# ScalarE and VectorE take the program's own order through the whole of a two-layer encoder kernel

## The chip, the cores and the metric

The kernel runs on one core of a Trainium2 chip. The metric is the device time of one execution in microseconds (us). Before the change it is 2368.7 us, the median of 3 runs (2365.86 to 2369.22). In the texts PE is TensorE (PEld its weight loads), DVE is VectorE, ACT is ScalarE, POOL is GpSimd and SP is the engine that issues the loads.

## What is computed

The input is 256 tokens of width 2048 in float32. Two layers run one after the other:

```
h = x
layer 0: h += windowed attention(rms_norm(h)) @ a_w_o     # 32 query heads of 64, 4 key heads, a sink logit, ALiBi, QK-norm
layer 1: h += differential attention(rms_norm(h)) @ b_w_o # 8 heads, each with two softmax maps of width 128
each:    h += (silu(g) * u) @ w_ffn_out,  [g, u] = rms_norm(h) @ w_ffn_in        # 5632 wide
         h += rms_norm(p[i] @ ple_w_proj) * sigmoid(rms_norm(h) @ ple_w_gate)
```

All weights (some 425 MB) are read once, and the result must be as exact as a float32 product.

## The kernel before

**Products.** A float32 operand is split in two parts, `hi` (rounded to the type that PE multiplies fast) and `lo` (the rest), and a product is three matmuls: x.hi with w.hi, x.lo with w.hi, x.hi with w.lo (`Group.tile`, L173; the matmul is L176). Weights come by DMA as `raw` tiles of 128 rows by 4 pieces of 256 columns, twice; `split_block` (L134 to L140) makes from half of one a `ws` tile: ACT casts `hi` (L138), DVE subtracts to get `lo` (L139). One `ws` tile serves 12 matmuls of 512 columns: two row blocks k, two token blocks m, three products. There are four `ws` buffers, and `Feed.next` (L198) keeps splits for four tiles emitted: when a tile is taken, the one three places on has just been written down in the program.

**Groups.** `Group.run` (L150) multiplies 16 row blocks (or fewer) into two PSUM tiles and then calls `done`. For queries and keys `done` is `qk_norm` (L367): squares on ACT (L374), sums on DVE (L375), a chain of seven small operations on POOL for the inverse root (L217 to L225, L378), and two multiplies on DVE that give `qn` (L388).

**Pieces.** What else a head needs is cut in pieces that `Flow` (L43) mixes into the stream of matmuls, a step after each matmul, each at a due time that a piece before has set: `to_pairs` (transposes, L398, then `qT` or `qk` split on ACT and DVE at L210 and L211), `scores` (L408), `exps` (L411 to L427: on DVE `sc`, L417, and `nm`, L419; on ACT two exponentials `e`, L423; on DVE `rd`, L426), `keys_first` (transposes of `e`, L437, then `wT` split at L206 and L207) and `weigh` (L521 in layer 0, L607 in layer 1). Layer 0 has 16 pairs of heads, each with two `exps` in a row (`AttentionA.heads`, L488). Layer 1 has 8 heads with two score maps each (`AttentionB.scores`, L571), taken in four rounds of two heads; the second map ends in a scaling on POOL (L582) and a sum on DVE (L584). PSUM tiles for pieces (`at`) come from a ring of four: scores of one pair can only start when DVE has read what stood there.

**Order.** PE's order is by hand for the whole program: it runs as the program emits it. ACT and DVE are by hand only up to the end of the first group (the `with` at L808); from L819 on a scheduler of the toolchain sets the order in which their instructions stand in their queues, as it does for POOL and SP throughout. On the chip each of these queues is taken in the order that stands there. `small_vectors` (L337) and `minus_lambda` (L351), both emitted early in the second group, turn small parameter vectors on PE and make one number for layer 1 with a matmul at L353.

Of the kernel before, what the change touches and what calls it, by code (L numbers as in the profile page):

```python
# [34 lines left out]
WS_BUFS = 4  # L35
# [50 lines left out]
def encoder(ctx: ExitStack, tc: tile.TileContext, x, p, attn_norm, ffn_norm, a_w_qkv, a_q_norm,  # L86
# [20 lines left out]
    flow = Flow()  # L107
# [535 lines left out]
    def project(w, os, norm):  # L643

        def done(half, s):
            def add(ps):
                add_to_h(ps, s)
                if half == 1:
                    norm.add(s, 3.0)
            return add  # L650
        n = KT // 2

        class Half:
            def __len__(self):
                return max(0, len(os) - n)

            def __getitem__(self, k):
                return os[n + k]
        return [Group(w, half * n * P, n, s, (os, Half())[half], done(half, s))
                for half in range(2) for s in range(NS)]  # L660
# [122 lines left out]
    groups = attn_a.groups() + project(a_w_o[0], attn_a.os, norm)  # L783
# [6 lines left out]
    feed = Feed(groups)  # L790
# [17 lines left out]
    with tc.manual_schedule(engines={mybir.EngineType.Activation, mybir.EngineType.DVE}):  # L808
# [6 lines left out]
        first_ps = groups[0].run(feed)  # L815
        for q in range(NS):
            feed.split()
            norm_a.stat.add([h[:, m, q * W:(q + 1) * W] for m in range(NM)])
    feed.ahead = WS_BUFS  # L819
    first_done(first_ps)  # L820
    flow.later(3.0, small_vectors)
    for g in groups[1:]:
        g.run(feed)
    flow.finish()
    phases.close()


# [49 lines left out]
```

## Time and profile before

| | |
|---|---|
| median of 3 runs | 2368.7 us |
| profiled execution, its own time | 2368.39 us |
| span of its trace, first to last instruction | 2366.6 us |
| PE busy | 2339.1 us, 99% |
| DVE busy | 1345.3 us, 57% |
| ACT busy | 1117.6 us, 47% |
| POOL busy | 138.6 us, 6% |
| layer 0 attention, in the trace | 28 to about 263 us |
| layer 1 attention, in the trace | about 1168 to 1470 us |

A busy PE is one with a matmul under way; matmuls overlap, so a busy stretch says only that PE had no empty time. The waits of an engine are listed by what ended them; a wait for several things is put down to the one that came last. The order in which instructions stand on an engine is printed from the built program and holds no time.

### The profile page before, as it was taken

What the parts mean: (1) busy time and instruction counts of PE and PEld (TensorE: products, weight loads), DVE (VectorE), ACT (ScalarE), POOL (GpSimd) and SP (SyncE); (2) the same over time, 40 slices, a digit from 0 to 9 for tenths busy, and PEclk for the clock granted to TensorE, in tenths of its full rate; (3) what the DMA queues carried; (4) which work ended last, traced back from release to release, by engine and by line L of the source; (5) the groups of instructions that cost most, each with busy time, mean ns of one, the idle gap of its engine ahead of it and who ended that gap; (6) DMA issues with size and microseconds to landing.
All of it is one profiled execution on the core that took longest, in us unless ns stands there. A gap on an engine that the chain in (4) does not pass through costs nothing.

```text
span 2366.6 us, 28473 instructions
## 1 busy us (share of the span) xinstructions
PE 2339.1 (99%) x10853; PEld 1920.7 (81%) x10853; DVE 1345.3 (57%) x1550; ACT 1117.6 (47%) x1551; POOL 138.6 (6%) x309
## 2 busy tenths in 40 slices
PE   8999999999999999999999999999999999999999
PEld 6777788888888888888888888888888888888887
DVE  5668655555555454566567667655545554454564
ACT  5555554444434434455455555544444434434453
POOL 1332000000000000000121120000000000000000
PEclk9999999999999999999999999999999999999999
DMA  6433455555555555555545445555555555555554
GB/s 236 143 107 107 165 182 191 188 196 187 193 185 191 192 188 192 193 178 184 194 159 178 162 168 193 178 187 184 200 184 201 183 195 192 189 189 196 180 196 141
DMA packets 121570, 428.72 MB, mean 181 GB/s; under 512 B 13552, under 2 KB 16728, under 8 KB 121176
## 3 DMA queue, kind: packets, MB, share of 16 engines
q1 hardware_dynamic: 121432, 426.89, 51.6%
q8 instruction: 85, 1.39, 0.2%
q14 instruction: 53, 0.43, 0.1%
HBM read 424.74 MB, written 2.10 MB: 180 GB/s over the span
## 4 chain that ended last, share of the span: by engine, by line
PE 96%; DVE 1%; DMA 1%; POOL 1%; ACT 1%; issue 1%; SPq 0%; DVEq 0%; ACTq 0%; POOLq 0%
PE mm L176 91%; PE at L408 1%; PE at L720 1%; PE at L269 1%; DMA h<-in_x_dram 1%; PE at L521 1%; PE at L437 1%; PE at L607 1%; PE at L398 0%; DVE ws L139 0%; POOL rs_y L219 0%; ACT ws L138 0%; DVE sc L417 0%; DMA raw<-in_a_w_qkv_dram 0%; DVE nm L419 0%
## 5 line engine op out<-in xcount | busy, mean ns | idle before, releaser
L176 PE MATMUL mm<-ws,xt 128*128 128x512 f32 x9600 | 2302.8, 397 | 6.1 <-DVE xt L207 4.2
L176 PEld LDWEIGHTS mm<-ws,xt 128*128 128x128 f32 x9600 | 1791.0, 188 | 405.8 <-DVE xt L207 5.4
L139 DVE TENSOR_TENSOR ws<-raw,ws 128x1024 fp32r<-128x1024 f32 x800 | 977.9, 1226 | 871.2 <-ACT ws L138 870.6
L138 ACT CAST ws<-raw 128x1024 fp32r<-128x1024 f32 x800 | 840.3, 1052 | 1035.9 <-PE mm L176 963.9
L217 POOL TENSOR_SCALAR rs_v<-ssum 128x2 f32<-128x2 f32 x8 | 1.5, 191 | 1708.0 <-DVE ssum L246 1708.0
L298 DVE TENSOR_TENSOR h<-mm,h 128x512 f32<-128x512 f32 x96 | 61.8, 682 | 1.5 <-PE mm L176 1.5
L210 ACT ACTIVATE xt<-at,gains 128x256 fp32r<-128x256 f32 x96 | 44.2, 473 | 33.1 <-DVE xt L211 23.9
L206 ACT CAST xt<-at 128x256 fp32r<-128x256 f32 x108 | 37.9, 372 | 42.7 <-DVE xt L207 31.8
L269 PE MATMUL at<-ident,h 128*128 128x128 f32 x192 | 52.6, 287 | 4.9 <-DMA h<-in_x_dram 4.8
L423 ACT ACTIVATE e<-sc,nm 128x257 f32<-128x257 f32 (+1 forms) x96 | 47.8, 501 | 15.4 <-DVE nm L419 15.4
L211 DVE SCALAR_TENSOR_TENSOR xt<-at,gains,xt 128x256 fp32r<-128x256 f32 x96 | 44.8, 480 | 17.9 <-ACT xt L210 17.9
L207 DVE TENSOR_TENSOR xt<-at,xt 128x256 fp32r<-128x256 f32 x108 | 43.2, 418 | 12.6 <-ACT xt L206 12.6
L521 PE MATMUL at<-wT,vp 128*128 128x256 f32 x192 | 47.4, 281 | 0.9 <-DVE sc L417 0.9
L720 PE MATMUL at<-ident,hid 128*128 128x128 f32 x176 | 47.8, 272 | 0.0
L219 POOL TENSOR_TENSOR rs_y<-rs_v,halves 128x2 f32<-128x2 f32 (+2 forms) x29 | 46.0, 1587 | 2.3
L437 PE MATMUL at<-ident,e 128*128 128x128 f32 x160 | 44.1, 277 | 0.0
L388 DVE TENSOR_TENSOR qn<-mm,rr 128x512 f32<-128x512 f32 (+1 forms) x28 | 16.9, 647 | 44.8 <-POOL rr L378 44.8
L701 ACT ACTIVATE silu<-mm,rinv 128x512 f32<-128x512 f32 x44 | 29.9, 688 | 19.7 <-PE mm L176 19.7
L521 PEld LDWEIGHTS at<-wT,vp 128*128 128x128 f32 x192 | 33.5, 189 | 1.8 <-ACT e L423 1.1
L501 POOL TENSOR_SCALAR e<-e,rd 128x256 f32<-128x256 f32 x64 | 33.6, 538 | 14.0 <-DVE rd L426 12.4
L269 PEld LDWEIGHTS at<-ident,h 128*128 128x128 f32 x192 | 27.7, 147 | 8.2 <-DMA h<-in_x_dram 5.4
L206 ACT CAST wT<-at 128x512 fp32r<-128x512 f32 x40 | 22.9, 580 | 23.5 <-PE at L437 23.4
(93 smaller groups left out, 652.0 us busy)
## 6 DMA issues: line engine op xcount, KB each, us to landing
raw<-in_w_ffn_in_dram SPq DMA_DIRECT2D x352, 512.0 KB
raw<-in_w_ffn_out_dram SPq DMA_DIRECT2D x176, 512.0 KB
raw<-in_b_w_qkv_dram SPq DMA_DIRECT2D x96, 512.0 KB
raw<-in_ple_w_gate_dram SPq DMA_DIRECT2D x64, 512.0 KB
raw<-in_a_w_qkv_dram SPq DMA_DIRECT2D x40, 512.0 KB
raw<-in_a_w_o_dram SPq DMA_DIRECT2D x32, 512.0 KB
raw<-in_b_w_o_dram SPq DMA_DIRECT2D x32, 512.0 KB
raw<-in_ple_w_proj_dram SPq DMA_DIRECT2D x16, 256.0 KB
```

Source lines behind the costliest of these rows:

```text
L138: nc.scalar.copy(out=ws[:, 0], in_=src)
L139: nc.vector.tensor_tensor(out=ws[:, 1], in0=src, in1=ws[:, 0].bitcast(F32), op=ALU.subtract)
L176: nc.tensor.matmul(ps[m], x[:, a, mslice(m)], w, start=(k == 0 and i == 0), stop=(k == self.n - 1 and i == 2))
L206: nc.scalar.copy(out=hi, in_=src)
L211: nc.vector.scalar_tensor_tensor(out=lo, in0=src, scalar=scale, in1=hi.bitcast(F32), op0=ALU.mult, op1=ALU.subtract)
L219: nc.gpsimd.tensor_tensor(out=y, in0=v, in1=halves[:, :n], op=ALU.pow)
L269: nc.tensor.transpose(ps[:, j, mslice(m)], h[:, m, (k + j) * P:(k + j + 1) * P], ident)
L298: nc.vector.tensor_tensor(out=hs, in0=ps[m], in1=hs, op=ALU.add)
L423: nc.scalar.activation(out=e[:, m, :], in_=sc[:, m, :], func=AF.Exp, bias=nm[:, m:m + 1], accum_out=den[:, m:m + 1])
L437: nc.tensor.transpose(ps[:, kh, mslice(m)], w[:, m, kh * P:(kh + 1) * P], ident)
L521: nc.tensor.matmul(ps, v[:, a, c0:c0 + P], wT[:, b, kh, :], start=(n == 0), stop=(n == 11))
L720: nc.tensor.transpose(ps[:, j, mslice(m)], hid[m][:, (j0 + j) * P:(j0 + j + 1) * P], ident)
```

## The change

The block in which ACT and DVE follow the program's order is carried on to the last instruction. Nothing that is computed changes, nor do the tiles, the buffers or the loads.

```
@@ -816,12 +816,12 @@
         for q in range(NS):
             feed.split()
             norm_a.stat.add([h[:, m, q * W:(q + 1) * W] for m in range(NM)])
-    feed.ahead = WS_BUFS
-    first_done(first_ps)
-    flow.later(3.0, small_vectors)
-    for g in groups[1:]:
-        g.run(feed)
-    flow.finish()
+        feed.ahead = WS_BUFS
+        first_done(first_ps)
+        flow.later(3.0, small_vectors)
+        for g in groups[1:]:
+            g.run(feed)
+        flow.finish()
     phases.close()
```

PE's order is the same in both. POOL's differs in one place (a scaling of `e` stands ahead of a root instead of behind it), SP's in the place of one load of layer 1. On ACT and DVE three places matter below.

The first is DVE behind the group of keys and values of layer 0, where `small_vectors` falls (`lp` is what the matmul at L353 reads). Before:

```order
L246 TENSOR_REDUCE ssum<-nss 128x2
L341 COPY gains<-at 128x64
L342 COPY cols<-at 128x10
L345 TENSOR_SCALAR gq_a<-cols 128x1
L345 TENSOR_SCALAR gq_b<-cols 128x1
L139 TENSOR_TENSOR ws<-raw,ws 128x1024
L375 TENSOR_REDUCE ss<-sq 128x4 x2
L345 TENSOR_SCALAR subln<-cols 128x2
L348 TENSOR_TENSOR lp<-cols 128x2
L388 TENSOR_TENSOR qn<-mm,rr 128x4x64 x4
```

There `lp` stands ahead of the multiplies `qn`. The same place of DVE after the change:

```order
L246 TENSOR_REDUCE ssum<-nss 128x2
L375 TENSOR_REDUCE ss<-sq 128x4 x2
L388 TENSOR_TENSOR qn<-mm,rr 128x4x64 x4
L211 SCALAR_TENSOR_TENSOR vp_436<-mm,rinv,vp_436 128x4x64
L211 SCALAR_TENSOR_TENSOR vp_440<-mm,rinv,vp_440 128x4x64
L139 TENSOR_TENSOR ws<-raw,ws 128x1024
L341 COPY gains<-at 128x64
L342 COPY cols<-at 128x10
L345 TENSOR_SCALAR gq_a<-cols 128x1
L345 TENSOR_SCALAR gq_b<-cols 128x1
L345 TENSOR_SCALAR subln<-cols 128x2
L348 TENSOR_TENSOR lp<-cols 128x2
```

Now `lp` and the copies it comes from stand behind `qn`, the two halves of the values (`vp`) and a weight split.

The second is DVE in layer 0 behind the second group of queries, with the scores of the second pair of heads. Before:

```order
L211 SCALAR_TENSOR_TENSOR qT<-at,gq_a,qT 128x2x256
L375 TENSOR_REDUCE ss<-sq 128x8 x2
L139 TENSOR_TENSOR ws<-raw,ws 128x1024
L388 TENSOR_TENSOR qn<-mm,rr 128x512 x2
L417 SCALAR_TENSOR_TENSOR sc<-dist,at 128x2x256 x2
L419 TENSOR_REDUCE nm<-sc 128x2 x2
L139 TENSOR_TENSOR ws<-raw,ws 128x1024
L426 RECIPROCAL rd<-den 128x2
L207 TENSOR_TENSOR wT<-at,wT 128x512
```

There a weight split stands in the gap ahead of `qn`, and both heads are read out of PSUM one right behind the other. The same place of DVE after the change:

```order
L211 SCALAR_TENSOR_TENSOR qT<-at,gq_a,qT 128x2x256
L375 TENSOR_REDUCE ss<-sq 128x8 x2
L388 TENSOR_TENSOR qn<-mm,rr 128x512 x2
L139 TENSOR_TENSOR ws<-raw,ws 128x1024
L417 SCALAR_TENSOR_TENSOR sc<-dist,at 128x2x256
L419 TENSOR_REDUCE nm<-sc 128x2
L426 RECIPROCAL rd<-den 128x2
L417 SCALAR_TENSOR_TENSOR sc<-dist,at 128x2x256
L419 TENSOR_REDUCE nm<-sc 128x2
L426 RECIPROCAL rd<-den 128x2
L139 TENSOR_TENSOR ws<-raw,ws 128x1024
L207 TENSOR_TENSOR wT<-at,wT 128x512 x2
```

The weight split has moved behind `qn`, and the second head's `sc` behind the first head's `rd`, which reads what ACT's exponentials of the first head leave.

The third is DVE in layer 1, where the second head of a round has its two score maps while the first head's `wT` is due. Before:

```order
L417 SCALAR_TENSOR_TENSOR sc<-dist,at 128x512 x2
L419 TENSOR_REDUCE nm<-sc 128x2 x2
L139 TENSOR_TENSOR ws<-raw,ws 128x1024
L426 RECIPROCAL rd<-den 128x2
L207 TENSOR_TENSOR wT<-at,wT 128x512
L426 RECIPROCAL rd<-den 128x2
L580 TENSOR_SCALAR r2l<-rd,nlam 128x2
L584 SCALAR_TENSOR_TENSOR e<-e,rd 128x256 x2
```

There `wT` stands between the two `rd`. The same place of DVE after the change:

```order
L417 SCALAR_TENSOR_TENSOR sc<-dist,at 128x512
L419 TENSOR_REDUCE nm<-sc 128x2
L426 RECIPROCAL rd<-den 128x2
L417 SCALAR_TENSOR_TENSOR sc<-dist,at 128x512
L419 TENSOR_REDUCE nm<-sc 128x2
L426 RECIPROCAL rd<-den 128x2
L580 TENSOR_SCALAR r2l<-rd,nlam 128x2
L584 SCALAR_TENSOR_TENSOR e<-e,rd 128x256 x2
L139 TENSOR_TENSOR ws<-raw,ws 128x1024
L207 TENSOR_TENSOR wT<-at,wT 128x512
```

Now `wT` stands behind both maps of the other head, their sum and a weight split; ACT's exponentials stand in the same way ahead of its half of `wT`.

## Rows read from the trace of the kernel before

**Rows 1.** The page, part 1: busy time, share and count by engine.
```profile
PE 2339.1 (99%) x10853; PEld 1920.7 (81%) x10853; DVE 1345.3 (57%) x1550; ACT 1117.6 (47%) x1551; POOL 138.6 (6%) x309
```

**Rows 2.** What PE waited for, 62 to 265 us: us, times, longest.
```profile
PE at L408 <- DVE xt L207: 4.5, 1, 4.5
PE mm L176 <- DVE xt L207: 4.2, 3, 2.6
```

**Rows 3.** Busy time by stretch (from:to, length; count of instructions behind x).
```profile
62.00:263.00 201.00, 186.61 (x1067) 149.26 (x1065) 141.91 (x219) 108.75 (x236) 60.40 (x122) 0.97 0.35 122
1168.00:1470.00 302.00, 301.97 (x1475) 249.71 (x1474) 201.63 (x273) 158.87 (x264) 48.35 (x113) 1.00 0.49 168
```

**Rows 4.** Groups by line and shape: busy us, mean ns of one.
```profile
L138 ACT CAST ws<-raw 128x1024 fp32r<-128x1024 f32 x800 | 840.3, 1052 | 1035.9 <-PE mm L176 963.9 <-issue 48.0 <-DVE sc L417 9.6
...
L211 DVE SCALAR_TENSOR_TENSOR v<-mm,rinv,v 128x256 fp32r<-128x256 f32 x16 | 7.3, 474 | 0.0
...
L211 DVE SCALAR_TENSOR_TENSOR qk<-at,cols,qk 128x512 fp32r<-128x512 f32 x8 | 6.0, 745 | 0.4 <-ACT qk L210 0.4
```

**Rows 5.** Instructions in time behind the first group: start, length, engine.
```profile
45.42 0.16 DVE L348 TENSOR_TENSOR lp<-cols 128x2 f32<-128x2 f32 x1
...
46.21 0.28 PE L353 MATMUL at<-lp,ones 128*128 128x2 f32 x2
...
48.88 1.42 DVE L388 TENSOR_TENSOR qn<-mm,rr 128x256 f32<-128x256 f32 x4 [3.31 <-POOL rr L378]
```

**Rows 6.** Instructions in time around the first query group's end.
```profile
59.69 15.38 PE L176 MATMUL mm<-ws,xt 128*128 128x512 f32 x67
...
63.84 1.23 DVE L139 TENSOR_TENSOR ws<-raw,ws 128x1024 fp32r<-128x1024 f32 x1 [0.25 <-ACT ws L138]
...
69.34 1.29 DVE L388 TENSOR_TENSOR qn<-mm,rr 128x512 f32<-128x512 f32 x2 [4.27 <-POOL rr L378]
```

**Rows 7.** Instructions in time at the second and third pair's scores.
```profile
94.14 1.29 DVE L388 TENSOR_TENSOR qn<-mm,rr 128x512 f32<-128x512 f32 x2 [4.58 <-POOL rr L378]
95.34 1.28 DVE L417 SCALAR_TENSOR_TENSOR sc<-dist,at 128x512 f32<-128x512 f32 x2
96.08 0.38 PE L408 MATMUL at<-kd,qT 64*128 64x256 f32 x1 [2.35 <-DVE sc L417]
...
97.31 0.51 ACT L423 ACTIVATE e<-sc,nm 128x257 f32<-128x257 f32 x1 [4.81 <-DVE nm L419]
...
98.22 0.18 ACT L423 ACTIVATION_READ_ACCUMULATOR e<-sc,nm 128x1 f32 x1
```

**Rows 8.** Busy time by stretch, for the granted clock (third number from the right).
```profile
96.50:100.00 3.50, 3.32 (x17) 2.71 (x18) 3.28 (x8) 2.69 (x10) 1.40 (x3) 0.68 0.00 0
100.00:104.00 4.00, 4.00 (x19) 3.32 (x19) 4.00 (x6) 2.40 (x8) 1.52 (x5) 0.86 0.00 0
...
135.50:139.00 3.50, 3.44 (x16) 2.81 (x17) 3.50 (x7) 0.00 (x0) 0.00 (x0) 0.50 0.00 0
139.00:143.00 4.00, 4.00 (x16) 2.87 (x15) 2.35 (x4) 2.20 (x5) 0.00 (x0) 0.61 0.00 0
...
180.00:184.00 4.00, 3.23 (x18) 2.61 (x19) 3.42 (x6) 1.83 (x3) 0.00 (x0) 1.00 0.28 67
```

**Rows 9.** Instructions in time in layer 1, second round.
```profile
1276.66 0.69 DVE L417 SCALAR_TENSOR_TENSOR sc<-dist,at 128x512 f32<-128x512 f32 x1 [0.44 <-PE at L408]
...
1282.72 0.94 POOL L582 TENSOR_SCALAR e<-e,r2l 128x256 f32<-128x256 f32 x2 [19.87 <-DVE r2l L580]
1283.24 1.09 DVE L584 SCALAR_TENSOR_TENSOR e<-e,rd 128x256 f32<-128x256 f32 x2 [0.30 <-POOL e L582]
...
1284.51 0.87 PE L408 MATMUL at<-qk,qk 128*128 128x256 f32 x6
...
1292.15 0.69 DVE L207 TENSOR_TENSOR wT<-at,wT 128x512 fp32r<-128x512 f32 x1
...
1292.89 0.38 PE L607 MATMUL at<-v,wT 128*128 128x256 f32 x1
```

## The prediction

> **What bounds the kernel now.** The page comes first: PE is busy for 2339.1 of 2366.6 us, DVE for little over half [rows 1]. So the change can only take away the few waits that PE has, or add new ones, and the second view is the list of PE's waits: in layer 0's attention it waits once for 4.5 us and three times, 4.2 us together, for an `xt` that DVE splits [rows 2]. The third view, busy time by stretch, tells where there is room. In layer 0's attention DVE works 141.9 of 201 us, at the granted clock of 0.97; in layer 1's PE works without a break [rows 3]. In the feed-forward stages, which the change leaves in nearly the same order (one `xt` moves past one weight split), I cost it at nothing: three tiles of splits lie ready there, 36 matmuls, and 67 matmuls run in 15.38 us [rows 6], 0.23 us each, so 8.2 us of cover.
>
> The fourth view is the instructions in time at the places where the order moves, and from it the durations are taken. The sum is made against the profiled execution's own 2368.4 us, 1.8 us more than its span and 0.3 us below the median of the runs.
>
> **The change, part by part.** Nothing is added but waiting. A queue that stands in the program's order meets each result at the moment it is made: DVE stands still while POOL makes a root and while ACT makes exponentials, and what would have filled the gap stands behind.
>
> *The start.* PE's matmul at L353 begins at 46.21, just after `lp` at 45.42 [rows 5]. Now `lp` stands behind `qn`, which ends at 48.88 + 1.42 = 50.30 because POOL makes the root until then [rows 5]. Behind it come the value halves (on ACT until about 50.8), the cast of a weight tile (1.05, [rows 4]) and its `lo` (1.23, as in [rows 6]), which ends at 53.1, and six small operations of about 0.15 (as `lp`, [rows 5]): 54.0. PE comes to L353 at the same time as before, so it waits 54.0 - 46.2 = 7.8 us. No other matmul stands between that could be done.
>
> *Layer 0's first query group.* The `lo` that ran at 63.84, in the gap before `qn`, now runs behind `qn`'s end at 70.63 and is there at 71.86 [rows 6]. The group ends near 61.7, the tile is due 36 matmuls later and its `lo` with the third product: 61.7 + 8.2 + 0.4 = 70.3. PE waits 1.6 us.
>
> *Layer 0's pairs of heads.* Before, both `sc` take 1.28 us together [rows 7], and both `nm` as much. Now the second head waits for the first: `sc` and `nm` 1.28, a step of 0.14, two exponentials from 97.31 to 98.40 [rows 7], 1.09, and `rd` with its step 0.28, 2.8 us for a head and 5.6 for a pair, against 2.9 of work: 2.7 us of standing still for each of 16 pairs. The first place where this reaches PE is the third pair's scores, which wait for the second pair's `sc` to leave PSUM and did so already before, until 96.08 [rows 7]. The first pair's 5.6 us hold ACT and so the next `qT`, the squares and with them `qn` by 2.3 us; with the 1.6 above `qn` ends at 95.43 + 3.9 = 99.3. Then a `lo` (1.2), the first head (2.8) and the second `sc` (0.64): 104.0, where it was 95.34 + 1.28 = 96.6 [rows 7]. That is 7.4 us, the 1.6 among them. Such a queue (two pairs' 2.7 and a `lo` of 1.2, 6.6 us) stands ahead of PE at four more places by the order and the waits: the scores that waited 4.5 us, and the three matmuls that waited for `xt`, the last at the end of the pairs [rows 2]. I take them all, 7.4 + 4 x 6.6 = 34 us. From below, all 16 x 2.7 = 43 us could fall into the 201 - 141.9 = 59 us in which DVE is idle [rows 3]; but those are partly waits that stay, so I put the low end at 15. From above, 43 and a `lo` of 1.2 for each of four groups: 48.
>
> *Layer 1's rounds.* Take the second. The first `sc` begins at 1276.66 as before [rows 9]. A head of 2.8, the weight cast and `lo` behind the exponentials (until about 1281.6), a head of 2.8, 0.2 for a small scaling, 0.5 for half of POOL's 0.94 and 1.09 for the sum [rows 9] make 1286.3, and then 0.75 for the other head's `qk` [rows 4]: 1287.1. PE's scores read it and began at 1284.51 [rows 9]: 2.6 us of wait. Then DVE has four values of 0.47 [rows 4], two `lo` of 1.23, the second of them held 0.5 by its cast, two heads of 2.8, 0.2 and 0.5 and 1.09, a `lo` and 0.69 for `wT` [rows 9]: about 1301.4. PE's second matmul of L607 wants `wT` and stood at 1292.89 [rows 9]: 8.5 us in all, the 2.6 among them. Four rounds make 34 us. The low end is the 2.6 alone, 10 us; the high end is 10.5 a round, should the exponentials' chain cost a microsecond more in each, 42.
>
> *The clock.* After the wait of 4.5 us the granted clock was 0.50 for 3.5 us and 0.61 for 4 us, of 2.4 GHz, so at the level of 1.2 for most of it; that cost 3.3 us [rows 8]. After the wait that ended at 96.08 it was 0.68 and 0.86, 1.7 us [rows 7, 8]. After one of the three `xt` waits, in 180 to 184 us, it stayed at 1.00 [rows 2, 8]. Five new long waits stand where nothing hides a slow PE, the start and four rounds of layer 1; at 1.7 to 3.3 us each, 2.5 in the middle, 12 us. The ends are 0 (none falls) and 9 falls of 3.3, 30. [...]
>
> Together 7.8 + 34 + 34 + 12 = 87.8 us: 2368.4 + 87.8, **2456 us**.
>
> What is taken away is small: the one wait that the new order might end is put in the second rival.
>
> **The rivals.** *First, layer 1 hides it.* If `wT` comes in time in layer 1, because ACT's and DVE's queues run ahead while PE works on, only the start, layer 0 and the 2.6 us a round are paid: 7.8 + 34 + 10 and one fall of the clock, 2.5, so 2368.4 + 54 = 2423. For it speaks that DVE is idle a third of that stage [rows 3]; against it, that `wT` was ready only 0.05 us before its matmul even when it stood ahead [rows 9].
>
> *Second, not slower.* DVE is idle 43% of the time [rows 1], and PE takes its work in just the order that ACT and DVE would now follow. If the scheduler's choices are what made PE wait for `xt` and `sc`, the program's order ends the 4.5, the 4.2 and the 2.4 us [rows 2, 7] and the two falls of the clock, 5.0: 16 us less, 2352. The point that decides is the place of `xt` against `qn` in DVE's queue: this case needs `xt` ahead of it. In the order printed above `qn` is still met at once and a `lo` has gone behind it, so I give it little. If waits of both signs cancel, the time is 2368.
>
> *Third, worse.* If PE, once slowed, is at the low clock through most of layer 0's pairs, and DVE's late `lo` also holds back the loads of `raw`, layer 0 costs its 48, layer 1 its 42 and the clock 30: 7.8 + 48 + 42 + 30 = 128, so 2496. Against it: a PE that is slow where DVE is the bound loses nothing.
>
> **How the numbers follow.** The forecast, between 2435 and 2480, 64%; layer 1 hides it, 14%; worse, 18%; not slower, 4%, of which I give 2 to faster and 2 to no change. A measurement of this kernel tells from no change what is beyond about 0.2%. So slower has 96%, no change 2%, faster 2%. The range goes from the first rival, less 8 us of the doubt in layer 0, 2415, to the third, 2496; outside it are the second rival and some tails of the others, some 2 in 10.
>
> **What would show it.** In the changed kernel's trace L353 should wait for `lp` for 7 to 8 us; the list of PE's waits should have at L607 a wait for `wT` of 5 to 6 us four times, and at L408 in layer 1 one for `qk` of 2 to 3 us four times; the reciprocals should have waits for `e` of over 1 us, nearly 48 times; the stretch of layer 0's attention should be longer by 40 to 45 us with the start, layer 1's by 34 to 45, the feed-forward stages by under 1. It is wrong if the feed-forward stages grow, if the waits at L607 are missing, or if layer 0's attention takes less than 20 us more.

## The result and the profile after

The changed kernel takes 2456.1 us (median of 4 runs, 2454.63 to 2456.97) against 2368.2 us (2365.86 to 2369.22) before: ratio 1.0369, 95% interval 1.0353 to 1.0384. That is 88 us more, slower, and the total forecast (2456) is met. The terms behind it are not: about 21 us that the prediction put down to waits are in fact a slower PE clock.

Part 1 of the page, the changed kernel, answers to [rows 1]:

```profile
PE 2371.7 (97%) x10853; PEld 1940.2 (79%) x10853; DVE 1355.4 (55%) x1550; ACT 1117.5 (46%) x1551; POOL 127.8 (5%) x309
```

The span went from 2366.6 to 2455.2 us, 88.6 more. PE does the same 10853 matmuls and is busy for 32.6 us more than in [rows 1]; the other 56.0 us it stands still. So two things grew: the waits, and the time that the same matmuls take. The mean granted clock fell from 0.997 to 0.983 of full speed. Half speed loses half of a stretch, so what is lost is the length times what is missing: 0.003 x 2366.6 = 7.1 us before, 0.017 x 2455.2 = 41.7 us after, 34.6 us more. That is the 32.6 us by which PE is busier, within the rounding of the clock.

The list of what PE waited for, whole span of the changed kernel (us, times, longest):

```profile
PE at L408 <- DVE qk L211: 8.8, 4, 2.2
PE at L607 <- DVE wT L207: 7.8, 4, 2.0
PE at L607 <- ACT wT L206: 7.5, 4, 3.1
PE at L408 <- DVE xt L207: 7.4, 1, 7.4
PE mm L176 <- DVE xt L207: 6.5, 2, 5.7
PE at L353 <- DVE lp L348: 6.5, 1, 6.5
...
PE mm L176 <- DVE ws L139: 4.5, 4, 1.3
PE at L408 <- DVE sc L417: 3.8, 3, 2.3
PE mm L176 <- ACT xt L206: 3.7, 3, 2.7
```

Against [rows 2], the two lines of waits for `xt` grew from 4.5 and 4.2 to 7.4 and 6.5 us; the waits for `lp`, `qk` and `wT` are new. So is one that the prediction had not looked for in layer 1: three weight splits of 1.3 us at L176.

The groups of instructions that stand still (busy us, mean ns of one, then the idle time ahead of them and what ended it), in the changed kernel:

```profile
L388 DVE TENSOR_TENSOR qn<-mm,rr 128x512 f32<-128x512 f32 (+1 forms) x28 | 16.9, 647 | 50.3 <-POOL rr L378 50.3
L426 DVE RECIPROCAL rd<-den 128x2 f32<-128x2 f32 x48 | 8.0, 166 | 56.5 <-ACT e L423 56.5
```

The same two groups in the kernel before:

```profile
L388 DVE TENSOR_TENSOR qn<-mm,rr 128x512 f32<-128x512 f32 (+1 forms) x28 | 16.9, 647 | 44.8 <-POOL rr L378 44.8
...
L426 DVE RECIPROCAL rd<-den 128x2 f32<-128x2 f32 x48 | 7.7, 160 | 10.4 <-ACT e L423 10.3
```

So `qn` stood still nearly as long before, with a weight split in the gap ahead of it at some places; what is new is the standing still ahead of `rd`. DVE now stands still before each `rd`, 56.5 / 48 = 1.18 us a time. The Trainium skill ("PSUM — Partial Sum Buffer", "Engine vs sequencer instructions") says that the queues of ACT, DVE and POOL are strictly first in, first out; these rows agree: DVE waits 1.18 us for the exponentials 48 times over, whatever stands behind `rd`.

The start, instructions in time of the changed kernel:

```profile
49.17 1.41 DVE L388 TENSOR_TENSOR qn<-mm,rr 128x256 f32<-128x256 f32 x4 [3.45 <-POOL rr L378]
...
53.72 0.15 DVE L348 TENSOR_TENSOR lp<-cols 128x2 f32<-128x2 f32 x1
...
54.02 0.56 PE L353 MATMUL at<-lp,ones 128*128 128x2 f32 x2 [6.49 <-DVE lp L348]
```

The chain is the one that was predicted, `qn`, values, a split, six small operations, and `lp` comes at 53.72 where it came at 45.42 [rows 5].

The first round of layer 1, instructions in time of the changed kernel:

```profile
1256.72 0.98 PE L408 MATMUL at<-qk,qk 128*128 128x256 f32 x6 [2.15 <-DVE qk L211]
...
1267.84 0.39 PE L607 MATMUL at<-v,wT 128*128 128x256 f32 x1 [1.45 <-ACT wT L206]
...
1270.39 0.39 PE L607 MATMUL at<-v,wT 128*128 128x256 f32 x1 [1.93 <-DVE wT L207]
...
1298.70 4.18 PE L176 MATMUL mm<-ws,xt 128*128 128x512 f32 x17 [1.32 <-DVE ws L139]
```

In [rows 9] `wT` was ready just as PE came; here it is late twice, once for ACT's half and once for DVE's.

Busy time by stretch (from:to, length; PE, PEld, DVE, ACT, POOL; the granted clock is the third number from the right):

```profile
54.00:60.50 6.50, 6.48 (x17) 5.20 (x18) 2.36 (x3) 1.22 (x2) 0.00 (x0) 0.53 0.48 163
...
60.00:320.00 260.00, 225.36 (x1179) 177.19 (x1179) 158.84 (x235) 120.78 (x254) 52.44 (x122) 0.91 0.30 107
320.00:1230.00 910.00, 910.00 (x4101) 749.32 (x4100) 493.30 (x512) 419.08 (x515) 17.25 (x33) 1.00 0.54 189
1230.00:1575.00 345.00, 316.89 (x1470) 258.65 (x1469) 204.99 (x274) 156.06 (x260) 41.05 (x112) 0.96 0.43 151
...
1256.00:1260.00 4.00, 3.28 (x17) 3.05 (x18) 3.40 (x7) 2.75 (x4) 0.00 (x0) 0.78 0.00 0
1260.00:1265.00 5.00, 5.00 (x22) 3.91 (x22) 3.77 (x7) 1.09 (x4) 0.00 (x0) 0.83 0.60 210
1265.00:1270.00 5.00, 2.01 (x9) 1.11 (x7) 3.12 (x7) 3.46 (x7) 0.93 (x2) 1.00 0.00 0
...
1273.00:1280.00 7.00, 7.00 (x31) 5.76 (x31) 2.29 (x4) 3.53 (x7) 1.68 (x6) 0.83 0.56 202
...
1298.00:1302.00 4.00, 3.30 (x14) 2.74 (x15) 3.46 (x5) 0.66 (x2) 0.00 (x0) 1.00 0.58 177
1343.00:1347.00 4.00, 3.96 (x16) 3.58 (x17) 3.40 (x6) 2.75 (x4) 0.00 (x0) 0.57 0.01 4
1347.00:1351.00 4.00, 4.00 (x22) 3.23 (x21) 2.71 (x6) 1.10 (x4) 0.00 (x0) 1.00 0.79 262
...
1429.50:1434.00 4.50, 4.50 (x28) 3.90 (x29) 3.90 (x7) 2.75 (x4) 0.00 (x0) 1.00 0.14 11
```

The feed-forward stage between the two attentions (320 to 1230) has no empty PE time and the full clock; behind layer 1's attention PE stands still for 5.2 us, where it was 5.1 before. In the attention stages the clock is 0.91 and 0.96, where it was 0.97 and 1.00 [rows 3]. In the round shown above it falls twice, behind the wait at L408 (0.78 and 0.83) and behind those at L607 (0.83).

### The profile page after: what moved, and what is told of

Read it like the earlier page. It is cut to its first block, busy times and chain, and to the rows that moved or that the text cites. A ratio compares the mean times of both kernels' runs of the same rounds, so it can differ in the third digit from the quotient of the medians.

```text
span 2455.2 us, 28431 instructions
## 1 busy us (share of the span) xinstructions
PE 2371.7 (97%) x10853; PEld 1940.2 (79%) x10853; DVE 1355.4 (55%) x1550; ACT 1117.5 (46%) x1551; POOL 127.8 (5%) x309
## 4 chain that ended last, share of the span: by engine, by line
PE 87%; DVE 6%; ACT 3%; POOL 2%; issue 1%; DMA 0%; SPq 0%; ACTq 0%; DVEq 0%; POOLq 0%
PE mm L176 83%; DVE ws L139 2%; ACT e L423 1%; ACT ws L138 1%; DVE nm L419 1%; POOL rs_y L219 1%; PE at L720 1%; PE at L269 1%; PE at L521 1%; DVE sc L417 1%; PE at L607 1%; DVE wT L207 0%; DVE ss L375 0%; PE at L437 0%; PE at L408 0%
## 5 line engine op out<-in xcount | busy, mean ns | idle before, releaser
L176 PE MATMUL mm<-ws,xt 128*128 128x512 f32 x9600 | 2325.5, 399 | 15.3 <-DVE xt L207 6.5
L176 PEld LDWEIGHTS mm<-ws,xt 128*128 128x128 f32 x9600 | 1803.3, 190 | 421.4 <-DVE xt L207 8.1
L521 PE MATMUL at<-wT,vp 128*128 128x256 f32 x192 | 50.0, 297 | 5.5 <-DVE wT L207 3.1
L242 ACT ACTIVATE sq<-h 128x512 f32<-128x512 f32 x48 | 30.0, 626 | 37.5 <-DVE h L298 31.1
L607 PE MATMUL at<-v,wT 128*128 128x256 f32 x96 | 31.5, 328 | 15.4 <-DVE wT L207 7.8
L388 DVE TENSOR_TENSOR qn<-mm,rr 128x512 f32<-128x512 f32 (+1 forms) x28 | 16.9, 647 | 50.3 <-POOL rr L378 50.3
L521 PEld LDWEIGHTS at<-wT,vp 128*128 128x128 f32 x192 | 35.8, 204 | 8.2 <-DVE wT L207 4.7
L426 DVE RECIPROCAL rd<-den 128x2 f32<-128x2 f32 x48 | 8.0, 166 | 56.5 <-ACT e L423 56.5
L219 POOL TENSOR_TENSOR rs_y<-rs_v,halves 128x2 f32<-128x2 f32 (+2 forms) x29 | 37.6, 1297 | 2.4
```

The lines of the kernel that those rows point to most:

```text
L176: nc.tensor.matmul(ps[m], x[:, a, mslice(m)], w, start=(k == 0 and i == 0), stop=(k == self.n - 1 and i == 2))
L219: nc.gpsimd.tensor_tensor(out=y, in0=v, in1=halves[:, :n], op=ALU.pow)
L521: nc.tensor.matmul(ps, v[:, a, c0:c0 + P], wT[:, b, kh, :], start=(n == 0), stop=(n == 11))
L607: nc.tensor.matmul(po[:, m, :], wT[:, a, kh, mslice(m)], vs[kh][:, b, :], start=(n == 0), stop=(n == 5))
```

## The experiments

Twelve kernels ran. Where a time is compared with the change, that is 2456.1 us; "before" was run again beside each group of them and took 2368.95 to 2369.45 us.

### Where the loss is made: one attention stage at a time

Layer 0 only (groups 1 to 12 inside the block, the rest outside):

```
+    with tc.manual_schedule(engines={Activation, DVE}):
+        first_done(first_ps)
+        flow.later(3.0, small_vectors)
+        for g in groups[1:13]:
+            g.run(feed)
+    for g in groups[13:]:
+        g.run(feed)
```

> ACT and DVE follow the program's order through layer 0's attention and its projection only; from the feed-forward stage on the scheduler sets the order again. My theory: the loss is made in the two attention stages and nowhere else, and each pays for its own. The last wait of layer 0's attention stands 45 us later in the changed trace (308.4 against 263.3), of which about 1 us was there before the change's first instruction: 44 us, so 2368 + 44 = 2412 us. Rival, the feed-forward stages pay too (their order differs in some fifty places): then this one and the next together stay well short of the change's 88 us. Rival, the loss in layer 1 comes from what layer 0 leaves behind: this one would be at 2440 or more.

Measured: 2413.0 us, ratio 1.0186 (1.0171 to 1.0201), 43.5 us more than before. Part 1 of its page:

```profile
PE 2356.2 (98%) x10853; PEld 1931.2 (80%) x10853; DVE 1349.2 (56%) x1550; ACT 1117.1 (46%) x1551; POOL 129.6 (5%) x309
```

PE is busy for 17.1 us longer than in [rows 1]: of the 43.5 us, some 17 are clock and the rest waits.

Layer 1 only, first with a block around each of its twenty groups:

```
     for i, g in enumerate(groups[1:], 1):
+        if first_b <= i < first_b + 20:
+            with tc.manual_schedule(engines={Activation, DVE}):
+                g.run(feed)
```

> ACT and DVE follow the program's order only in layer 1's attention and its projection (and up to the end of the first group, as before). My theory: what the change costs there it costs alone, four rounds of about 11 us as in the changed trace (a round took 75.4 us and takes 86 to 88): 44 us, 2412 us, with the same waits at L408 (2.2 us), L607 (about 3.4 us a round) and at the weights (1.3 us), and PE's clock below full in the same stretch. Rival, feed-forward stages pay too: below 2400, with this and the layer 0 one together under 80 us of loss.

Measured: 2395.5 us, 1.0112 (1.0095 to 1.0128), 26 us instead of 44. The theory's number fell, but so did the premise: with a block around each group, splits of the next group had slipped forward into the gaps of the one before. DVE's order against that of the whole change, in one round:

```
-L388 TENSOR_TENSOR qn<-mm,rr 128x512 x2
-L139 TENSOR_TENSOR ws<-raw,ws 128x1024 x6
...
+L139 TENSOR_TENSOR ws<-raw,ws 128x1024
+L388 TENSOR_TENSOR qn<-mm,rr 128x512 x2
+L139 TENSOR_TENSOR ws<-raw,ws 128x1024 x5
...
+L139 TENSOR_TENSOR ws<-raw,ws 128x1024
+L419 TENSOR_REDUCE nm<-sc 128x2
+L139 TENSOR_TENSOR ws<-raw,ws 128x1024
 L426 RECIPROCAL rd<-den 128x2
```

The same stage inside one block tells the two readings apart:

```
+    with tc.manual_schedule(engines={Activation, DVE}):
+        for g in groups[first_b:first_b + 20]:
+            g.run(feed)
```

> As the layer 1 run before, but with one block around the twenty groups of layer 1's attention and projection instead of a block around each. With a block around each, weight splits had come to stand in DVE's gaps (between the sums and qn, between nm and rd), and the run lost only 26 us; with one block ACT's and DVE's order in this stage is that of the change to the last instruction. My theory: the place of the weight splits is what made the difference, so this one loses 42 to 46 us, 2412 us, and with layer 0's 43.5 the change's 88 us are accounted for. Rival, the feed-forward stages or what layer 0 leaves behind make the missing 18 us: this one stays at 2395.

Measured: 2413.6 us, 1.0188 (1.0173 to 1.0203), 44.3 us more than before. So 43.5 + 44.3 = 87.8 of the 88 us are the two attention stages, each paid by itself (each of the two known to some 4 us), and nothing is left for the feed-forward stages. And 18 us of layer 1's 44 hang on nothing but the place of some weight splits. Part 1 of the page of the run with one block:

```profile
PE 2355.0 (98%) x10853; PEld 1931.0 (80%) x10853; DVE 1348.5 (56%) x1550; ACT 1116.8 (46%) x1551; POOL 131.2 (5%) x309
```

PE's wait for ACT's half of `wT` in that run:

```profile
PE at L607 <- ACT wT L206: 9.1, 4, 3.1
```

The same wait in the run with twenty blocks:

```profile
PE at L607 <- ACT wT L206: 1.1, 1, 1.1
```

Layer 1's clock costs 2355.0 - 2339.1 = 15.9 us. With the splits in the gaps ACT's half of `wT` is late once instead of four times, while the wait for `qk` is longer, 11.6 us instead of 8.8. PE is busy for 2346.3 us in that run, so 8.7 of the 18 us are clock.

### Which queue: one engine at a time

DVE alone, then ACT alone, in the program's order to the end:

```
+    with tc.manual_schedule(engines={mybir.EngineType.DVE}):
```

> Only DVE follows the program's order to the end; ACT's is set by the scheduler, as before. My theory: the loss is made in DVE's queue, where lp stands behind qn, the second head's sc behind the first one's rd, and wT and the weight splits behind those; ACT only waits for it. So nearly all of it is here: 75 to 90 us, 2443 to 2458 us. Rival, both queues share it (the exponentials of the second head, and ACT's half of wT, behind each other): about 44 us, 2412. Rival, ACT's order is what costs: within 15 us of 2368.

Measured: 2459.1 us, 1.0381 (1.0366 to 1.0397), 89.6 us more than before: with DVE in the program's order, and ACT left to the scheduler, the whole loss is there. What PE waited for most:

```profile
PE at L607 <- DVE wT L207: 19.8, 4, 5.0
```

```
+    with tc.manual_schedule(engines={mybir.EngineType.Activation}):
```

> Only ACT follows the program's order to the end; DVE's is set by the scheduler, as before. My theory: ACT's order then costs little, since both sc and both nm of a pair are made one behind the other again and its four exponentials follow without a gap; what is left is ACT's half of wT behind the exponentials in layer 1 and of qT in layer 0: 0 to 20 us, 2368 to 2388 us. Rival, both queues share it: about 44 us, 2412. Rival, ACT's order is what costs: 2440 or more.

Measured: 2399.3 us, 1.0131 (1.0115 to 1.0146), 30 us. That is 10 us more than I gave it at most. It is not the price of ACT's order by itself, though, because the scheduler did not put DVE back into the order of before. DVE in this run, in the first round of layer 1:

```profile
1230.90 0.17 DVE L426 RECIPROCAL rd<-den 128x2 f32<-128x2 f32 x1 [1.09 <-ACT e L423]
...
1232.01 1.08 DVE L584 SCALAR_TENSOR_TENSOR e<-e,rd 128x256 f32<-128x256 f32 x2 [0.68 <-POOL e L582]
1233.02 1.21 DVE L139 TENSOR_TENSOR ws<-raw,ws 128x1024 fp32r<-128x1024 f32 x1
1234.16 0.68 DVE L207 TENSOR_TENSOR wT<-at,wT 128x512 fp32r<-128x512 f32 x1
```

Here `wT` stands behind both `rd`, the sum and a weight split, as in the third place of the change, and PE waits 7.8 us for it in four rounds, as much as in the change. Nor is ACT's order in the run with DVE alone that of before: exponentials and casts stand otherwise. So the two runs (90 and 30, together 88) do not split the loss between the queues; what either order costs with the other as it was before stays open.

### Which wait: one place at a time

Each of the next four is the whole change with one place written otherwise. First, PE asks for `lp` later:

```
-        flow.later(4.0, lambda: minus_lambda(lp))
+        flow.later(14.0, lambda: minus_lambda(lp))
```

> The whole change, and minus_lambda is due 14 us after small_vectors instead of 4, so PE meets L353 some 10 us later, when lp is long there. My theory: PE's wait of 6.5 us at L353 is a loss by itself, and the clock that stood at 0.53 for the 6.5 us behind it costs another 3: 2456 - 9.5 = 2446.5 us, between 2445 and 2451. Rival, DVE is the one that is behind there, and PE only meets its lateness at the next place (the first query group's weight splits or the keys' transposes): within 3 us of 2456.

Measured: 2449.6 us, 1.0337 (1.032 to 1.0354), 6.5 us less than the change, inside the theory's bounds but less than its 9.5. The wait at L353 is gone from the list and PE is busy for 3.6 us less:

```profile
PE 2368.1 (97%) x10853; PEld 1938.1 (79%) x10853; DVE 1355.6 (55%) x1550; ACT 1117.2 (46%) x1551; POOL 127.4 (5%) x309
```

About 6.5 + 3.6 = 10 us are won at the start, and some 4 us of them come back, most of it where PE, now earlier, meets DVE in the pairs of layer 0: the waits for `sc` are 5.1 us instead of 3.8, those for `wT` at L521 4.5 instead of 3.1.

Second, the weight split in the gap ahead of `qn`:

```
                                 in1=rinv.unsqueeze(2).broadcast_to([P, NM, nh]), op=ALU.mult)
+        if len(feed.ready) < WS_BUFS:
+            feed.split()
         outs = []
```

> The whole change, and qk_norm writes the next weight split down between the root on POOL and the multiplies qn, where the scheduler had put it; nothing else moves. My theory: DVE and ACT stand still there for the root (4 us) with a split of 1.2 us due behind it, twice a round in layer 1 and once for each of five groups in layer 0: 4 x 2 x 1.2 = 10 in layer 1, 4 in layer 0, and two falls of the clock less, 3 each: 2456 - 20 = 2436 us, between 2430 and 2446. Rival, the splits in the gap between nm and rd are what matters and this one not: within 4 us of 2456.

Measured: 2451.2 us, 1.0345 (1.033 to 1.0361), 5 us less than the change: nearer to the rival than to the 20 us of the theory, and outside the bounds of both. The wait of 4.5 us for `ws` falls to 0.5, and that is about all:

```profile
PE mm L176 <- DVE ws L139: 0.5, 1, 0.5
```

So the waits for weights are this gap's doing; the rest of the 18 us that the twenty blocks had kept would then lie in the splits between `sc`, `nm` and `rd`, or in those behind the values. No run separated these.

Third, the two heads of a pair of layer 0 written down together, `sc`, `nm`, `sc`, `nm`, four exponentials, both `rd`:

```
+            ins = [exps_in(ps[e2], ...) for e2, hd in enumerate(hs)]
+            mid = [exps_e(i) for i in ins]
             for e2 in range(2):
-                e, rd = exps(ps[e2], ...)
+                e, rd = exps_out(mid[e2])
```

> The whole change, and in layer 0 the two heads of a pair are written down together: sc, nm, sc, nm, then four exponentials, then both rd. My theory: a pair then stands still once for the exponentials instead of twice, 1.4 us less for each of 16 pairs, and PSUM is read 1.5 us sooner; of the 34 us that layer 0 lost without the start some 15 come back: 2441 us, between 2431 and 2448. Rival, what costs in layer 0 is qn standing ahead of splits, not the heads: within 4 us of 2456.

Measured: 2436.7 us, 1.0286 (1.027 to 1.0301), 19.5 us less than the change. The reciprocals' idle time fell from 56.5 to 36.6 us:

```profile
L436 DVE RECIPROCAL rd<-den 128x2 f32<-128x2 f32 x48 | 7.8, 162 | 36.6 <-ACT e L429 36.6
```

That is 19.9 us less standing still on DVE for 19.5 us less in all, of which PE's busy time makes 10.4 (2361.3 us) and its waits the rest. The two numbers agree with a layer 0 in which what DVE stands still is paid, in waits and in clock; that they must be equal is not shown.

Fourth, the same in layer 1, with `rd` and the sum 2.5 us behind the exponentials:

```
             if c == 1:
+                flow.later(2.5, lambda: self.join(hd, s))
+
+        def join(self, hd, s):
...
-                flow.later(9.0, lambda: self.turn(hd, e1))
+                flow.later(6.5, lambda: self.turn(hd, e1))
```

> The whole change, and in layer 1 the two rd, the scaling and the sum of a head are written down 2.5 us behind its second map's exponentials (the turn 6.5 us behind them instead of 9), so that the other head's qk and wT come to stand ahead of them on DVE. My theory: in layer 1 PE waits for qk and wT because they stand behind the rd, which stand still for ACT: the waits for qk (8.8 us) go, of those for wT (15.3 us) at least 10, and some 8 of the 16 us of clock: 2456 - 27 = 2429 us, between 2420 and 2437. Rival, wT is held by ACT's casts and DVE's splits, not by the rd: only the qk waits go, 2445 to 2449.

Measured: 2448.5 us, 1.0338 (1.0321 to 1.0356), 7.6 us less: the rival. PE's waits:

```profile
PE at L621 <- ACT wT L206: 15.5, 4, 3.9
...
PE at L408 <- DVE qk L211: 2.5, 4, 0.6
PE at L621 <- DVE wT L207: 1.9, 4, 0.8
```

The waits for `qk` went, from 8.8 to 2.5 us, and DVE's half of `wT` is nearly in time, but the whole wait has moved to ACT's half. My reading, that the two `rd` were what held `wT`, does not stand.

### The clock by itself

The whole change, with 26 matmuls ahead of L353 whose result is overwritten:

```
+        xs = norm_a.xs
+        for _ in range(26):
+            nc.tensor.matmul(ps.rearrange("p a t -> p (a t)"), xs[0][:, 0, 0:P],
+                             xs[1].rearrange("p a t -> p (a t)"), start=True, stop=True)
```

> The whole change, and PE gets 26 matmuls of 512 columns ahead of L353 whose result is overwritten at once (6.0 us at the full clock, where it stands still for 6.5 us). My theory: the clock behind a wait is low because PE stood still; with the stand filled the granted clock behind 54 us is 1.00 where it was 0.53 for 6.5 us, and PE wins 3 us there, of which a part comes back as waits for DVE in the next groups, as with the late minus_lambda: 2453 us, between 2450 and 2457. Rival, the clock is low there for another reason: 0.5 to 0.6 in that stretch still, and 2456 us or more.

Measured: 2453.3 us, 1.0356 (1.0341 to 1.0372). By time alone this is not told apart from the change, but the stretch behind L353 is:

```profile
54.00:60.50 6.50, 6.32 (x29) 5.25 (x30) 3.63 (x6) 2.27 (x3) 0.00 (x0) 1.00 0.48 165
```

With the stand filled the clock is at 1.00 where it was 0.53, and PE gets 29 matmuls done in the stretch where it got 17. So the low clock behind L353 is a consequence of PE having stood still. And what PE wins there it keeps: its waits behind are as long as in the change, and come some 2.7 us earlier. At the third pair's scores in this run, and then in the change:

```profile
109.59 1.64 PE L412 MATMUL at<-kd,qT 64*128 64x256 f32 x11 [2.32 <-DVE sc L421]
...
112.31 1.64 PE L408 MATMUL at<-kd,qT 64*128 64x256 f32 x11 [2.31 <-DVE sc L417]
```

The part that was expected to come back as waits for DVE did not.

### Everything written down where it is due

The four places together (with `qn` 4.5 us behind its sums and layer 0's `rd` 2 us behind the exponentials), still in the program's order:

```
-        flow.later(4.0, lambda: minus_lambda(lp))
+        flow.later(14.0, lambda: minus_lambda(lp))
...
+        flow.later(4.5, scale)
...
+            flow.later(2.0, lambda: self.scale(j, mid))
...
+                flow.later(2.5, lambda: self.join(hd, s))
```

> Program's order on ACT and DVE to the end, but each result is written down where it is due and not where it is asked for: minus_lambda 14 us behind small_vectors, the multiplies qn 4.5 us behind their sums, the heads of a pair of layer 0 together and their rd 2 us behind the exponentials, the rd and the sum of layer 1 2.5 us behind. My theory: the loss is nothing but results written down too early for a queue that is taken in order, so nearly all 88 us come back: 2370, between 2358 and 2385. Rival, the scheduler's order carries more than these four places (the place of every weight split): 2390 or more. If DVE's few waits of before in layer 0 go too, it is faster than before: under 2362.

Measured: 2406.0 us, 1.0155 (1.014 to 1.017). Of the 88 us, 50 come back and 37 stay: the rival. The idle time of `rd` is 2.2 us (it was 56.5) and that of `qn` 15.0 (50.3), so standing still for a result is not what is left. What is left in layer 1, instructions in time in its first round:

```profile
1220.71 2.36 DVE L139 TENSOR_TENSOR ws<-raw,ws 128x1024 fp32r<-128x1024 f32 x2 [0.45 <-ACT ws L138]
1222.98 0.68 DVE L421 SCALAR_TENSOR_TENSOR sc<-dist,at 128x512 f32<-128x512 f32 x1
...
1224.42 0.51 ACT L431 ACTIVATE e<-sc,nm 128x256 f32<-128x256 f32 x1 [2.79 <-DVE nm L423]
...
1226.73 1.03 ACT L138 CAST ws<-raw 128x1024 fp32r<-128x1024 f32 x1
1227.67 0.57 ACT L206 CAST wT<-at 128x512 fp32r<-128x512 f32 x1
...
1228.29 0.39 PE L627 MATMUL at<-v,wT 128*128 128x256 f32 x1 [3.89 <-ACT wT L206]
```

ACT's half of `wT` stands behind a cast and the other head's exponentials; those wait 2.79 us for `nm`, and `sc` and `nm` stand behind two weight splits, 2.36 us together. The splits that no one waits for yet are ahead of the scores that the next step waits for.

The last run makes PE ask later for what comes late there, and in layer 0 for the first scores of a group:

```
-                flow.later(2.0 + 8.6 * i, ...)
+                flow.later(4.0 + 7.0 * i, ...)
...
-                flow.later(6.5, lambda: self.turn(hd, e1))
+                flow.later(10.0, lambda: self.turn(hd, e1))
...
-            flow.later(3.5, lambda: self.weigh_when_ready(hd, got[0]))
+            flow.later(6.0, lambda: self.weigh_when_ready(hd, got[0]))
```

> As the run with everything written down where it is due, and PE asks later in two more places: in layer 1 for e (the turn 10 us behind the sum instead of 6.5) and for wT (weigh 6 us behind the turn instead of 3.5), in layer 0 for the first pair's scores of a qT (4 us instead of 2; the second 11 instead of 10.6). In the run before, PE waited in each round 3.9 us for ACT's half of wT and 0.8 us for DVE's: it stands behind the other head's four exponentials, which wait for two weight splits and sc and nm. My theory: PE has other matmuls to do there, so asking later costs nothing and the four waits (18 us) go with the clock that falls behind them (some 8 of the 15 us of clock): 2406 - 26 = 2380 us, between 2368 and 2390. Rival, the round is as long as DVE's queue in program's order makes it, and the wait comes back at the next place that asks (scores for qk, e, the weights): 2395 to 2406.

Measured: 2397.7 us, 1.0121 (1.0104 to 1.0138): 8.4 us won of the 26, and within the rival's bounds. ACT's 15.6 us of wait are gone, and DVE's have taken the place of half of them:

```profile
PE at L627 <- DVE wT L207: 9.5, 4, 2.4
```

No version here beats the kernel before. Of the last 29 us, 12.0 are PE's busy time (2351.1 us in this run's trace) and 13.8 are waits in layer 1, for `wT`, `qk` and `qn`. What makes these late was not found; the place of the weight splits is the suspect, since moving some of them was worth 18 us in layer 1, but no run moved them in this version.

## Why the prediction was right

The direction, the total and the stages were right, the stages shown by running each alone. By its own terms:

| term | predicted | measured |
|---|---|---|
| the start, wait for `lp` | 7.8 | 6.5 |
| layer 0's attention, waits | 34 | about 20 |
| layer 1's rounds, waits | 34 | 28 |
| the clock | 12 | 33 |
| feed-forward | 0 | 0 |

The measured waits are those of the list after, less those of the list before: in layer 0, without `lp`, 34 against 15 us; in layer 1 8.8 + 7.8 + 7.5 and the three splits, 4, against none. The terms add up to 87.5 us.

*The start* was right in its mechanism: `lp` came at 53.72 + 0.15, forecast 54.0. PE itself reached L353 1.3 us later than in [rows 5], most of it from loads of `h` that landed later, so the wait is 6.5 us.

*Layer 0.* The mechanism is shown: `rd` waits 1.18 us 48 times, and writing the heads of a pair down together gave back 19.5 us. The sizes were not met. The last wait at the third pair's scores, in the kernel before:

```profile
96.68 0.97 PE L408 MATMUL at<-kd,qT 64*128 64x256 f32 x11 [0.22 <-DVE sc L417]
```

In the changed kernel it ends at 112.31, 15.6 us later, close to the forecast 7.8 + 7.4 = 15.2. But that 15.6 is made of other parts: 6.5 at L353, 1.3 of PE's later start, 5.2 of a slower PE (busy for 47.56 us from 46.21 to 96.68 before, for 52.75 us from 54.02 to 112.31 now), and only some 2.6 of new waits where 7.4 were put. So the step "I take them all, 7.4 + 4 x 6.6 = 34 us" was too large at each of its places: at the four later ones the waits grew by 2.9 us (4.5 to 7.4), by 2.3 (4.2 to 6.5) and, where ACT's half of `xt` came last, by 2.2 (1.5 to 3.7), where 4 x 6.6 was put. About half of layer 0's 20 us are waits at places that the sum did not name.

The missing waits and the clock that came instead are of one size, 14 us each. That a slow PE comes later to the place where DVE is late, and so waits less, is not shown. The late `lp` speaks for it, with PE earlier and new waits; the filled wait speaks against it, with PE earlier and the same waits. The split at the first query group, put at 1.6 us, held PE neither in the change nor with the clock at 1.00 in the fill run.

*Layer 1.* The wait for `qk` was forecast at 2.6 us a round and is 2.2. The one for `wT` was forecast at 5.9 and is 3.4 to 5.0. What the prediction left out are the weight splits at the ends of three query and key groups, 1.3 us each: it had seen that a split goes behind `qn` in layer 0 and did not carry it to layer 1. As for what holds `wT`, it named the heads' standing still and the splits together; the runs show that the standing still can be taken away with the wait still there (15.5 us for ACT's half), and that moving splits takes 18 us off.

*The clock* is the term that was mis-sized: 12 us forecast, 33 measured, just past the 30 that it gave as the upper end. The step that failed is the count, "five new long waits". Layer 1 alone cost 15.9 us, 4 a round where 2.5 were put: each round has two places where the clock can fall, behind L408 and behind L607, and it fell at seven of these eight (not behind L408 in the third round, 1.00 from 1429.50). And layer 0 cost 17.1 - 3.1 for the start (0.47 x 6.5) = 14 us where the sum had nothing, because PE is in and out of short waits there and the clock stays at 0.91 over 260 us. The sentence against the third rival, that a slow PE loses nothing where DVE is the bound, does not hold here: the busy time grew in layer 0, and the 2.7 us that the fill run won on it at the start were still won at the end.

So that the total came out to the microsecond is luck: some 21 us too much of waits met 21 us too little of clock, and nothing in the working foresaw that they would cancel.

The row at 1.00 in [rows 8] was a poor guide to the sum: together the new waits cost 33 us of clock, though not each of them, since behind the 1.32 us at 1298.70 and the 2.22 us at 1429.45 it stayed at 1.00. The Trainium skill ("TensorE: Matmul & The Clock Gate", "Why this matters for your kernels") warns that a long idle gap between bursts of matmuls puts the clock back to half. The trace agrees at the 6.49 us ahead of L353, with 0.53 behind them, and shows 0.57 behind the shorter 2.22 us before 1343.04.

The rivals: layer 1 hid nothing (44.3 us), the waits that the second rival wanted ended (4.5, 4.2 and 2.4 us) are there still (7.4, 6.5 and 2.3), and the third rival's terms (48, 42 and 30) stayed out of reach, except its 30 for the clock.

## What to carry to other kernels

On engines whose queue is taken in order, the order of emission must place each instruction near the time at which its inputs are ready: write down other work between a request to another engine and the instruction that reads the answer, and put work with slack (here weight splits) into that gap rather than ahead of what the next step waits for. A profile that shows an engine half idle does not say that its order has room. When waits are added to a busy PE, count the matmul time at the lower clock as a term of its own, and not a small one: here it was 33 us beside 56 us of waits.

## What the runs showed of the hardware that was not expected

A wait of 2.22 us before 1343.04 was followed by a clock of 0.57 for 4 us and 1.00 in the 4 us behind, while the wait of 1.32 us before 1298.70 left it at 1.00. The same wait one round later, 2.22 us at the same instruction before 1429.45, left it at 1.00 too. In the kernel before, a wait of 2.65 us at 180.77 left it at 1.00 [rows 8], so the length of a wait alone does not tell whether the clock falls. Filling a wait with matmuls that compute nothing needed kept the clock at 1.00 and made the run no longer: its median is 2.8 us lower, as much as 12 matmuls of 0.23 us, the number by which its stretch behind L353 has more, though the two intervals overlap.
